# Down-projections of three feed-forward stages: seven block products per four hidden chunks in place of eight

## The chip, the core and the metric

One core of a Trainium2 chip. Its engines are PE (TensorE, the matmuls), DVE (VectorE), ACT (ScalarE), POOL (GpSimd) and SP (SyncE, which here issues the transfers of the weights). The metric is the device time of one launch in microseconds, as the median of the runs.

## What is computed

A stack of three layers over 512 tokens of width 1024, all in fp32. Each layer is a token mixer and then a feed-forward stage, with residuals and root-mean-square norms between. The change bears on the feed-forward stages and on the product `mod`:

```python
def _squared_relu_mlp(x, w1, w2):          # layers 0 and 1: w1 1024x4096, w2 4096x1024
    h = jax.nn.relu(x @ w1)
    return (h * h) @ w2

def swiglu(h, w_ffn_in, w_ffn_out):        # third layer: 1024x5632, 2816x1024
    gate, up = jnp.split(h @ w_ffn_in, 2, axis=-1)
    return (jax.nn.silu(gate) * up) @ w_ffn_out

c_act = jax.nn.silu(c)                     # c 1x1024, for the third layer
mod = c_act @ w_ada[l] + b_ada[l]          # w_ada 1024x6144
```

## The kernel before

**Products.** Every fp32 product runs as three matmuls: each operand is split into a rounded part (hi) and the rest (lo), and `mm3` (L277) issues hi·hi, hi·lo and lo·hi, lines L280 to L282:

```python
mm(out, s[0], m[0], start=start, stop=False)
mm(out, s[0], m[1], start=False, stop=False)
self.gemm = mm(out, s[1], m[0], start=False, stop=stop).ins
```

**Weights.** They come in units of 128x1024 (512 KB) in the order that `plan()` writes down. `unit` (L255) loads one by SP into a tile `wraw`, casts it on ScalarE into `whi` (L267) and subtracts on VectorE into `wlo` (L268). The tiles come from three rings, `RINGS` (L220): 3 raw, 4 hi and 4 lo, from a point in the first mixer on 3 more of hi and lo. A load waits until the subtraction on its slot's last content is through.

**A feed-forward stage** (`ffn`, L1149, for l = 0 and 1). The hidden width of 4096 is taken as 32 chunks of 128, in eight groups of four. `w1()` makes a group: for each chunk 24 matmuls into one PSUM bank (tile `g`; chunk-major, weights stationary), a relu with a scale per token on VectorE (L1168, `g` to `r`), a square on ScalarE (L1169), and `split` into hi and lo (ScalarE L274, VectorE L275) in the tile `a`. `accum_group` (L1190) then adds the group's share of the output into `m` (512 tokens x 1024): for each of two column halves two weight units, for each of four token tiles one bank (tile `a`) of 12 matmuls, which ScalarE copies out in the first group (L1198) and VectorE adds in all others (L1200). The loop makes group g and then projects group g-1 down, so TensorE has 96 matmuls up, 96 down in one round. The last group is projected by `tail`, whose evacuation is woven with the norms that follow.

**The modulation** (`modulation`, L1204) is done beside the first feed-forward stage alone, in seven steps of six or seven tiles of `w_ada` (48 in all, tile `wada`, two buffers of their own): SP loads 512 KB, and VectorE multiplies with `ca` and sums along the row in one instruction (L1220).

**The third stage** (`swiglu`, L1613) has 22 chunks in groups of 2, 4, 4, 4, 4, 4; a chunk takes two units of weights up (a gate and a value). While its last but one group is projected, GpSimd multiplies and adds finished halves of `m` into the residual (`gated`, L1636).

**PSUM** gives the products of these stages four banks, two named `g` and two `o`, taken in turn (`bank`).

**Order.** Each engine runs its own instructions strictly in order. These orders are set when the program is built, by a scheduler that goes by its estimates and the dependences; `issue_after(done)` (L1178) keeps the modulation's loads behind a relu of the round before.

## Time and profile before

| | |
|---|---|
| median of 3 runs | 2073.69 us (2072.18 to 2075.59) |
| profiled execution: its time | 2073.41 us |
| profiled execution: its span | 2071.6 us |
| granted TensorE clock, mean | 0.99 |

The profile shows one execution. Its page gives the busy time of each engine, the chain of work that ended last and the costliest groups of instructions; the trace behind it has the start and the duration of each instruction, what it waited for, and the busy time of each engine in any stretch. In the names, `a<-r` reads "tile a out of tile r", and `x64` counts instructions. Two matmuls after each other overlap in the records, so that the time between their starts, not their durations, tells how fast TensorE goes. A granted clock of 1.00 is the full 2.4 GHz, and the lower level is 1.2 GHz.

### The profile page before, as it was taken

Reading aid. Unit: us, or ns where it says so; the run is one execution under the profiler, and the core shown is the slowest. Engines: PE = TensorE matmul, PEld = TensorE weight load, DVE = VectorE, ACT = ScalarE, POOL = GpSimd, SP = SyncE. Lnnn points to the kernel's source line nnn. Section 1 sums busy time; section 2 is a strip of 40 time slices with the busy share of each in tenths; the row PEclk is TensorE's granted clock in tenths of the full one; section 3 lists DMA queues with packets and bytes.
Section 4 is the critical chain, followed back from the end, with each engine's and each line's share of the span. In section 5 each row is a group of like instructions: output and inputs, shape, how many; then the busy total and the mean of one; then the engine's idle time right before and its main releaser. Section 6 shows DMA issues by size and latency. Waiting matters only on the chain.

```text
span 2071.6 us, 26020 instructions
## 1 busy us (share of the span) xinstructions
PE 2026.2 (98%) x10312; PEld 1713.2 (83%) x10312; DVE 1113.7 (54%) x1698; ACT 801.9 (39%) x1352; POOL 189.5 (9%) x230
## 2 busy tenths in 40 slices
PE   8989999999999999999999999999999999999998
PEld 6767889888888788888888888898888889888886
DVE  7676656666665546665444444633564654243335
ACT  5445555422333534224432322424655434322222
POOL 3212221000002100003000000300000000000006
PEclk9989999999999999999999999999999999999999
DMA  7211043755542332222333223122121222323231
GB/s 251 85 31 42 31 156 110 240 189 196 190 148 77 115 101 94 93 85 72 102 102 102 92 92 102 62 93 91 49 75 62 90 93 92 102 92 98 89 99 41
DMA packets 59691, 213.54 MB, mean 103 GB/s; under 512 B 6952, under 2 KB 7273, under 8 KB 59185
## 3 DMA queue, kind: packets, MB, share of 16 engines
q1 hardware_dynamic: 56592, 202.84, 29.8%
q0 software_dynamic: 1728, 5.28, 0.8%
q10 hardware_dynamic: 1248, 3.76, 0.6%
q8 instruction: 81, 1.33, 0.3%
q14 instruction: 42, 0.34, 0.0%
HBM read 206.59 MB, written 2.10 MB: 101 GB/s over the span
## 4 chain that ended last, share of the span: by engine, by line
PE 90%; DVE 4%; POOL 3%; ACT 2%; issue 1%; DMA 0%; POOLq 0%; SPq 0%; ACTq 0%; DVEq 0%
PE g L280 13%; PE g L282 13%; PE g L281 13%; PE a L282 8%; PE a L280 8%; PE a L281 8%; PE h L281 2%; PE h L280 2%; PE h L282 2%; PE t L280 2%; PE t L281 2%; PE t L282 2%; PE l L280 2%; PE l L282 2%; PE l L281 2%
## 5 line engine op out<-in xcount | busy, mean ns | idle before, releaser
L267 ACT CAST whi<-wraw 128x1024 fp32r<-128x1024 f32 x326 | 340.9, 1048 | 851.3 <-PE g L281 385.3
L268 DVE TENSOR_TENSOR wlo<-wraw,whi 128x1024 fp32r<-128x1024 f32 x326 | 400.6, 1231 | 312.9 <-ACT whi L267 309.2
L280 PE MATMUL g<-a,whi 128*128 128x512 f32 x1200 | 474.3, 395 | 0.0
L281 PE MATMUL g<-a,whi 128*128 128x512 f32 x1200 | 470.5, 392 | 0.0
L282 PE MATMUL g<-a,wlo 128*128 128x512 f32 x1200 | 470.5, 392 | 0.0
L280 PE MATMUL a<-whi,a 128*128 128x512 f32 x688 | 268.3, 390 | 0.0
L281 PE MATMUL a<-wlo,a 128*128 128x512 f32 x688 | 267.8, 389 | 0.0
L282 PE MATMUL a<-whi,a 128*128 128x512 f32 x688 | 267.8, 389 | 0.0
L282 PEld LDWEIGHTS g<-a,wlo 128*128 128x128 f32 x1200 | 226.3, 189 | 46.9
L280 PEld LDWEIGHTS g<-a,whi 128*128 128x128 f32 x1200 | 226.8, 189 | 45.5 <-DVE a L1595 0.2
L281 PEld LDWEIGHTS g<-a,whi 128*128 128x128 f32 x1200 | 226.5, 189 | 45.1
L1200 DVE TENSOR_TENSOR a<-a,a 128x512 f32<-128x512 f32 x168 | 114.4, 684 | 104.1 <-PE a L282 103.6
L282 PEld LDWEIGHTS a<-whi,a 128*128 128x128 f32 x688 | 129.2, 188 | 26.8
L281 PEld LDWEIGHTS a<-wlo,a 128*128 128x128 f32 x688 | 129.2, 188 | 26.6
L280 PEld LDWEIGHTS a<-whi,a 128*128 128x128 f32 x688 | 129.2, 188 | 26.5
L280 PE MATMUL h<-a,whi 128*128 128x256 f32 x384 | 109.9, 290 | 4.4 <-DVE a L540 2.7
L281 PE MATMUL h<-a,whi 128*128 128x256 f32 x384 | 109.8, 287 | 2.2 <-DVE a L597 2.0
L282 PE MATMUL h<-a,wlo 128*128 128x256 f32 x384 | 109.4, 286 | 0.0
L1168 DVE SCALAR_TENSOR_TENSOR r<-g,rbc 128x512 f32<-128x512 f32 x52 | 35.9, 691 | 128.5 <-PE g L282 128.5
L280 PE MATMUL l<-whi,a 128*128 128x512 f32 x256 | 100.8, 394 | 0.0
L282 PE MATMUL l<-whi,a 128*128 128x512 f32 x256 | 99.6, 390 | 0.0
L281 PE MATMUL l<-wlo,a 128*128 128x512 f32 x256 | 99.5, 389 | 0.0
(411 smaller groups left out, 2795.7 us busy)
## 6 DMA issues: line engine op xcount, KB each, us to landing
wraw<-wbig SPq DMA_DIRECT2D x320, 512.0 KB, 3.5
wada<-wada SPq DMA_DIRECT2D x48, 512.0 KB, 4.5
cw<-cmp_w SPq DMA_DIRECT2D x2, 1024.0 KB, 10.2
rowng<-rows POOLq DMA_DIRECT2D x4, 512.0 KB, 5.2
h<-x ACTq DMA_DIRECT2D x1, 2048.0 KB, 11.3
out<-a SPq DMA_DIRECT2D x8, 256.0 KB, 2.2
xin<-xT SPq DMA_DIRECT2D x3, 512.0 KB, 7.4
qt<-qt ACTq DMA_DIRECT2D x12, 128.0 KB, 2.2
```

The source lines that it names most:

```text
L267: nc.scalar.copy(hi[:, :w], raw)
L268: nc.vector.tensor_tensor(lo[:, :w], raw, hi[:, :w].bitcast(F32), ALU.subtract)
L280: mm(out, s[0], m[0], start=start, stop=False)
L281: mm(out, s[0], m[1], start=False, stop=False)
L282: self.gemm = mm(out, s[1], m[0], start=False, stop=stop).ins
L1168: done = nc.vector.scalar_tensor_tensor(r, o, 0.0, rb, ALU.max, ALU.mult).ins
L1200: nc.vector.tensor_add(t, t, o)
```

## The change

Four hidden chunks (a group) times 1024 columns are a product of two by two blocks: tokens in two halves of 256 by hidden chunks in two pairs, and hidden pairs by column halves. Strassen's scheme in Winograd's form takes seven block products and block sums where the plain way takes eight. The class `Winograd` does this for a stage:

- The hidden blocks stay F32 in a region `ys` (two groups); blocks and their sums are split into a ring of four slots of hi and lo.
- The seven products run in the order 1: a11·b11, 2: a12·b21, 5: s1·t1, 3: s4·b22, 6: s2·t2, 7: s3·t3, 4: a22·t4, each of two banks with six matmuls per bank. Each product has an accumulator of 128x2x512: four lie in `m`, and products 1, 6 and 7 have tiles of their own (`acc`).
- The sums of hidden blocks (s1 to s4, tile `yt`, 128x512) and of weight blocks (t1 to t4, tile `wt`, 128x1024) run on GpSimd, from the raw tiles. The casts and subtractions of the weights follow on these sums.
- After the last group but one, `join` forms the result's blocks from the accumulators, with five sums on GpSimd and two on VectorE; the last group of each stage is still projected by `tail` in the plain way. In the third stage the groups are 4, 4, 4, 4, 2, 4, and `group` serves the first four; the group of two runs as before.
- The modulation's tiles come from the raw ring and have no `issue_after`. Its product is a GpSimd multiplication and a ScalarE copy that sums along the row.
- The rings of hi and lo grow by 2 in place of 3, and the raw ring grows from 3 to 5.

```diff
-RINGS = (("raw", 3), ("hi", 4), ("lo", 4)), (("hi", 3), ("lo", 3))
+RINGS = (("raw", 3), ("hi", 4), ("lo", 4)), (("raw", 2), ("hi", 2), ("lo", 2))
...
             for g in range(1, 8):
-                *yn, after = w1()
-                self.accum_group("w2", y, m, g == 1)
-                y = yn
+                w1(g)
+                down.group(g - 1, g == 7)
                 if l == 0:
-                    with tc.issue_after(done):
-                        self.modulation(g)
-                done = after
+                    self.modulation(g)
...
         for j in range(lo, hi):
-            w = self.ada.tile([P, D], F32, tag="w", name="wada")
+            w = self.turned("raw").tile([P, D], F32, tag="w", name="wada")
             nc.sync.dma_start(w, a["wada"][j])
-            nc.vector.scalar_tensor_tensor(w, w, 1.0, self.ca, ALU.mult, ALU.mult, accum_out=self.mod[:, j:j + 1])
+            nc.gpsimd.tensor_tensor(w, w, self.ca, ALU.mult)
+            nc.scalar.activation(w, w, AF.Copy, accum_out=self.mod[:, j:j + 1])
...
+class Winograd:
...
+    def group(self, g, last):
+        k, nc = self.k, self.k.nc
+        y = self.y(g)
+        a11, a12, a21, a22 = (y[:, 2 * c:2 * c + 2, i * 256:i * 256 + 256] for i in range(2) for c in range(2))
+
+        def sub(a, b, n, op=ALU.subtract):
+            t = self.temp(self.wk, "yt" if n == 256 else "wt", n)
+            nc.gpsimd.tensor_tensor(t, a, b, op)
+            return t
+
+        def product(p, a, b):
+            a, b = self.pair(a), k.parts(b)
+            for i in range(2):
+                o = k.bank(k.ps, f"a{p}{i}_")
+                for _ in k.token_major(o, [([b], Kernel.stationary(a))], i):
+                    pass
+                t = self.acc[p][:, i]
+                if g == 0:
+                    nc.scalar.copy(t, o)
+                else:
+                    nc.vector.tensor_add(t, t, o)
+
+        b11, b21 = k.raw_unit(self.tag), k.raw_unit(self.tag)
+        s1 = sub(a21, a22, 256, ALU.add)
+        product(1, a11, b11)
+        s2 = sub(s1, a11, 256)
+        product(2, a12, b21)
+        b12 = k.raw_unit(self.tag)
+        t1 = sub(b12, b11, 512)
+        product(5, s1, t1)
+        s4 = sub(a12, s2, 256)
+        b22 = k.raw_unit(self.tag)
+        t2 = sub(b22, t1, 512)
+        product(3, s4, b22)
+        product(6, s2, t2)
+        s3 = sub(a11, a21, 256)
+        t3 = sub(b22, b12, 512)
+        t4 = sub(t2, b21, 512)
+        product(7, s3, t3)
+        product(4, a22, t4)
+        if last:
+            self.join()
+
+    def join(self):
+        nc, acc = self.k.nc, self.acc
+        nc.gpsimd.tensor_tensor(acc[2], acc[2], acc[1], ALU.add)
+        nc.gpsimd.tensor_tensor(acc[6], acc[6], acc[1], ALU.add)
+        nc.gpsimd.tensor_tensor(acc[7], acc[7], acc[6], ALU.add)
+        nc.vector.tensor_tensor(acc[6], acc[6], acc[5], ALU.add)
+        nc.vector.tensor_tensor(acc[3], acc[3], acc[6], ALU.add)
+        nc.gpsimd.tensor_tensor(acc[4], acc[7], acc[4], ALU.subtract)
+        nc.gpsimd.tensor_tensor(acc[5], acc[5], acc[7], ALU.add)
```

How the orders of the engines change is shown for a late round of the first stage, in which the weight blocks are `wraw_5324` (b11), `wraw_5326` (b21), `wraw_5376` (b12) and `wraw_5404` (b22). Line numbers are those of the kernel named.

GpSimd, the change, one round: `yt` are sums of hidden blocks, `wt_5378` is t1, `wt_5406` t2, `wt_5454` t3, `wt_5456` t4, and `wada` the modulation's products.

```order
L1736 TENSOR_TENSOR yt_5328<-a_3543 128x512
L1736 TENSOR_TENSOR yt_5352<-yt_5328,a_3543 128x512
L1736 TENSOR_TENSOR yt_5402<-a_3543,yt_5352 128x512
L1736 TENSOR_TENSOR wt_5378<-wraw_5376,wraw_5324 128x1024
L1736 TENSOR_TENSOR wt_5406<-wraw_5404,wt_5378 128x1024
L1736 TENSOR_TENSOR wt_5454<-wraw_5404,wraw_5376 128x1024
L1226 TENSOR_TENSOR wada<-wada,ca 128x1024 x2
L1736 TENSOR_TENSOR yt_5452<-a_3543 128x512
L1226 TENSOR_TENSOR wada<-wada,ca 128x1024 x2
L1736 TENSOR_TENSOR wt_5456<-wt_5406,wraw_5326 128x1024
L1226 TENSOR_TENSOR wada<-wada,ca 128x1024 x3
L1736 TENSOR_TENSOR yt_5667<-a_3543 128x512
```

Before, GpSimd has no instruction in such a round. Now it has eight sums and seven products, all seven products behind t2 and the last three behind t4.

ScalarE, before, the same place (casts of the down weights, squares, and the hi part of hidden chunks):

```order
L267 CAST whi_5322<-wraw_5321 128x1024
L1169 ACTIVATE r<-r 128x512
L274 CAST a_5017<-r 128x512
L267 CAST whi_5358<-wraw_5357 128x1024
L1169 ACTIVATE r<-r 128x512
L274 CAST a_5017<-r 128x512
L267 CAST whi_5394<-wraw_5393 128x1024
```

ScalarE, the change, the same round (L1227 are the copies that sum the modulation's products, L1180 the squares, L272 the casts of weight blocks and sums):

```order
L1227 ACTIVATE wada,mod<-wada 128x1024 x2
L272 CAST whi_5382<-wt_5378 128x1024
L1180 ACTIVATE a_3543<-a_3543 128x512
L1227 ACTIVATE wada,mod<-wada 128x1024 x3
L272 CAST whi_5410<-wraw_5404 128x1024
L1180 ACTIVATE a_3543<-a_3543 128x512
L1227 ACTIVATE wada,mod<-wada 128x1024 x2
L272 CAST whi_5432<-wt_5406 128x1024
L1180 ACTIVATE a_3543<-a_3543 128x512
L272 CAST whi_5460<-wt_5454 128x1024
```

The seven copies of one round stand ahead of the cast of that round's t2; the last two of them stand directly ahead of it. They read the seven GpSimd products of the fence above: before this cast ScalarE has 41 copies in its order, and GpSimd has 34 products ahead of t2 and 41 behind the round's last.

VectorE, the change, from the lo part of t2 on (L1179 relu, L273 lo of a weight, L281 lo of a hidden block, L1749 additions from PSUM):

```order
L273 TENSOR_TENSOR wlo_5433<-wt_5406,whi_5432 128x1024
L1179 SCALAR_TENSOR_TENSOR a_3543<-g_79_5297,rbc_2972 128x512
L273 TENSOR_TENSOR wlo_5461<-wt_5454,whi_5460 128x1024
L1749 TENSOR_TENSOR acc_37_3546<-acc_37_3546,a_81_5336 128x512
L1749 TENSOR_TENSOR acc_37_3546<-acc_37_3546,a_81_5344 128x512
L281 TENSOR_TENSOR a_3544<-yt_5352,a_3544 128x512
L273 TENSOR_TENSOR wlo_5483<-wt_5456,whi_5482 128x1024
L1749 TENSOR_TENSOR a_3545<-a_3545,a_81_5360 128x512
L1749 TENSOR_TENSOR a_3545<-a_3545,a_81_5368 128x512
L281 TENSOR_TENSOR a_3544<-yt_5452,a_3544 128x512
L1749 TENSOR_TENSOR a_3545<-a_3545,a_82_5386 128x512
L273 TENSOR_TENSOR wlo_5534<-wraw_5531,whi_5533 128x1024
```

It goes on with two additions, a split, the lo part `wlo_5567` of the second up-weight, two additions and the lo part `wlo_5600` of the third up-weight of the next round; the slot that `wlo_5600` reads, `wraw_5597`, is the one into which the next round's b22 is loaded. Before, the lo parts of the down weights stood in VectorE's order beside the modulation's own products (L1220) and waited for casts of raw units alone. On PE the order has 9395 rows before and 9179 with the change.

## Rows read from the trace of the kernel before

**Rows 1.** The page, section 1: busy time, share of the span and instructions of each engine.

```profile
PE 2026.2 (98%) x10312; PEld 1713.2 (83%) x10312; DVE 1113.7 (54%) x1698; ACT 801.9 (39%) x1352; POOL 189.5 (9%) x230
```

**Rows 2.** The page, section 4: the chain that ended last, by engine.

```profile
PE 90%; DVE 4%; POOL 3%; ACT 2%; issue 1%; DMA 0%; POOLq 0%; SPq 0%; ACTq 0%; DVEq 0%
```

**Rows 3.** Timeline, VectorE: start us, us, engine line op out<-in [idle before <-releaser].

```profile
481.43 0.69 DVE L1168 SCALAR_TENSOR_TENSOR r<-g,rbc 128x512 f32<-128x512 f32 x1 [2.76 <-PE g L282]
...
524.95 0.69 DVE L1168 SCALAR_TENSOR_TENSOR r<-g,rbc 128x512 f32<-128x512 f32 x1 [2.76 <-PE g L282]
```

**Rows 4.** Busy time by stretch: one period of the first feed-forward stage.

```profile
core 0: us, PE busy (x) PEld busy (x) DVE busy (x) ACT busy (x) POOL busy (x), PEclk, DMA share, GB/s
481.43:524.95 43.52, 43.52 (x193) 36.05 (x192) 27.96 (x40) 13.05 (x17) 0.00 (x0) 1.00 0.54 179
```

**Rows 5.** Groups by form, VectorE: line engine op, shapes xcount | busy us, mean ns | idle before.

```profile
L268 DVE TENSOR_TENSOR wlo<-wraw,whi 128x1024 fp32r<-128x1024 f32 x320 | 395.0, 1237 | 309.6 <-ACT whi L267 305.9
L1200 DVE TENSOR_TENSOR a<-a,a 128x512 f32<-128x512 f32 x168 | 114.4, 684 | 104.1 <-PE a L282 103.6
L1220 DVE SCALAR_TENSOR_TENSOR wada<-wada,ca 128x1024 f32<-128x1024 f32 x48 | 58.0, 1221 | 16.4 <-DMA wada<-wada 16.1
L275 DVE TENSOR_TENSOR a<-r,a 128x512 fp32r<-128x512 f32 x64 | 45.9, 725 | 1.2 <-ACT a L274 1.2
L1168 DVE SCALAR_TENSOR_TENSOR r<-g,rbc 128x512 f32<-128x512 f32 x52 | 35.9, 691 | 128.5 <-PE g L282 128.5
```

**Rows 6.** Groups by form, ScalarE.

```profile
L267 ACT CAST whi<-wraw 128x1024 fp32r<-128x1024 f32 x320 | 336.0, 1052 | 847.2 <-PE g L281 384.9 <-PE a L282 292.6 <-issue 66.3
L1169 ACT ACTIVATE r<-r 128x512 f32<-128x512 f32 x64 | 39.6, 625 | 4.2 <-DVE r L1168 4.2
L274 ACT CAST a<-r 128x512 fp32r<-128x512 f32 x64 | 39.3, 620 | 1.7
L494 ACT ACTIVATE junk<-h 128x1024 bf16<-128x1024 f32 x20 | 21.2, 1058 | 53.7 <-DVE h L551 38.2 <-DVE h L1607 12.7 <-issue 2.7
...
L494 ACT ACTIVATION_READ_ACCUMULATOR junk<-a 128x1 f32 x32 | 6.1, 190 | 0.0
```

**Rows 7.** Groups by form, GpSimd.

```profile
L1638 POOL TENSOR_TENSOR a<-a,row 128x512 f32<-128x512 f32 x8 | 10.3, 1290 | 319.7 <-DVE a L1200 319.6
...
L1237 POOL TENSOR_TENSOR ws<-ws,consts 128x1024 f32<-128x1024 f32 x1 | 2.4, 2387 | 3.9 <-DMA ws<-wsT 3.9
```

**Rows 8.** DMA issues: KB each, median us to landing.

```profile
wraw<-wbig SPq DMA_DIRECT2D x320, 512.0 KB, 3.5
wada<-wada SPq DMA_DIRECT2D x48, 512.0 KB, 4.5
```

**Rows 9.** Timeline, VectorE and GpSimd around 677 us.

```profile
677.14 2.35 DVE L268 TENSOR_TENSOR wlo<-wraw,whi 128x1024 fp32r<-128x1024 f32 x2
...
677.37 3.27 POOL L547 TENSOR_TENSOR mg<-a,rowng 128x512 f32<-128x512 f32 x1 [2.67 <-DVE a L540]
...
679.57 2.16 DVE L268 TENSOR_TENSOR wlo<-wraw,whi 128x1024 fp32r<-128x1024 f32 x1
...
680.61 2.24 POOL L554 TENSOR_TENSOR a<-a,rowng 128x512 f32<-128x512 f32 x1
```

**Rows 10.** Timeline, VectorE and GpSimd around 2045 us.

```profile
2044.88 1.28 POOL L1639 TENSOR_TENSOR h<-h,a 128x512 f32<-128x512 f32 x1
...
2044.98 1.73 DVE L1651 TENSOR_TENSOR h<-h,a 128x512 f32<-128x512 f32 x1
...
2046.79 1.29 POOL L1653 TENSOR_TENSOR a<-h,rownfin 128x512 f32<-128x512 f32 x1 [0.63 <-DVE h L1651]
...
2046.98 0.69 DVE L1650 TENSOR_TENSOR a<-l,row 128x512 f32<-128x512 f32 x1 [0.27 <-PE l L282]
```

**Rows 11.** Busy time by stretch, with PEclk, where TensorE had little to do.

```profile
83.00:87.00 4.00, 1.28 (x5) 1.10 (x6) 3.75 (x14) 2.21 (x8) 3.49 (x10) 0.88 0.01 4
87.00:91.00 4.00, 4.00 (x14) 3.22 (x14) 2.78 (x6) 1.20 (x3) 2.68 (x4) 0.69 0.30 74
```

More of the change, by code (lines that the diff above doesn't have):

```diff
@@ L149, in fi @@
             split4("fi", "w_ffn_in_2", 0, np.concatenate([_r(0), _r(DFF), _r(P), _r(DFF + P)]))
-            return
-        for i in range(4 * g - 2, 4 * g + 2):
+        for i in ((2, 3), range(4, 8), range(8, 12), range(12, 16), (16, 17), range(18, 22))[g]:
             fm("fg", "w_ffn_in_2", 0, _r(i * P))
@@ L513, in mod_row @@
     def mod_row(self, k, pool=None):
-        g = (pool or self.rows).tile([P, D], F32, tag="row", name=f"row{k}")
+        g = (pool or self.rows).tile([P, D], F32, tag="row", name=f"row{k}", bufs=1)
         for c in range(2):
@@ L1189, in accum_group @@
         nc = self.nc
+        kc, y = y[0].shape[1], self.stationary(y)
         for c in range(2):
-            ws = [self.unit(tag) for _ in range(y[0].shape[1] // 2)]
+            ws = [self.unit(tag) for _ in range(kc // 2)]
             for i in range(NT):
@@ L1639, in gated @@
                 nc.gpsimd.tensor_tensor(self.h[:, i, cs], self.h[:, i, cs], m[:, i, cs], ALU.add)
[L1641 removed]
+            fi(0)
             for g in range(1, 6):
[L1643 to L1645 removed]
+                fi(g)
+                if g < 5:
+                    down.group(g - 1, g == 4)
+            self.accum_group("fo", down.pairs(4, 2), m, False, gated)
             ss, col = self.cols4("ssm"), self.cols4("col")
@@ L1664, in swiglu @@
             ws = [[self.unit("fo") for _ in range(2)] for c in range(2)]
+            y = down.whole(5)
             tail = self.tail([(c, [(ws[c], y)]) for c in range(2)], evac)
@@ L1668, in swiglu, with __init__, block, y @@
                     pass
+class Winograd:
+    def __init__(self, k, wk, region, tag):
+        self.k, self.wk, self.tag = k, wk, tag
+        self.ys = k.region(region, F32)
+        self.ring = k.region(region)
+        self.slot = 0
+        self.m = k.tokens()
+        def block(i, c):
+            return self.m[:, 2 * i:2 * i + 2, c * 512:c * 512 + 512]
+        self.acc = {2: block(0, 0), 3: block(0, 1), 4: block(1, 0), 5: block(1, 1)}
+        for p in (1, 6, 7):
+            self.acc[p] = wk.tile([P, 2, 512], F32, name=f"acc{p}_{k.pos}", bufs=1)
+    def y(self, g):
+        return self.ys[:, 4 * (g % 2):4 * (g % 2) + 4]
+    def pair(self, src):
+        s = self.slot
+        self.slot = (s + 1) % 4
+        hi, lo = self.ring[:, s], self.ring[:, 4 + s]
+        if len(src.shape) == 3:
+            hi, lo = (t.rearrange("p (k t) -> p k t", k=src.shape[1]) for t in (hi, lo))
+        self.k.split(hi, lo, src)
+        return hi, lo
+    def pairs(self, g, n):
+        y = self.y(g)
+        self.slot = 0
+        for i in range(n):
+            self.pair(y[:, i])
+        return self.ring[:, :n], self.ring[:, 4:4 + n]
+    def whole(self, g):
+        y = self.y(g)
+        ps = [self.pair(y[:, i]) for i in range(4)]
+        return lambda k, i: tuple(t[:, i * P:(i + 1) * P] for t in ps[k])
+    def temp(self, pool, tag, n):
+        return pool.tile([P, 2, n], F32, tag=tag, name=f"{tag}{self.k.pos}", bufs=3)
+    def group(self, g, last):
+        k, nc = self.k, self.k.nc
+        y = self.y(g)
+        a11, a12, a21, a22 = (y[:, 2 * c:2 * c + 2, i * 256:i * 256 + 256] for i in range(2) for c in range(2))
[43 more added lines that the diff above has]
+        nc.gpsimd.tensor_tensor(acc[5], acc[5], acc[7], ALU.add)
```

83 lines of the change are left out of this document (40 added, 43 removed).

## The prediction, made before the changed kernel was run

> **What bounds the kernel now.** I read the page first: TensorE is busy for 98% of the span [rows 1], and the chain that ended last is 90% PE [rows 2]. So the question for any edit is what it does to the number of matmuls, and whether TensorE is still fed. Then I read one steady period of the first feed-forward stage (four hidden chunks up, four down). The evictions of the same unit in two following periods start at 481.43 and 524.95 [rows 3], 43.52 us apart. In this period 192 matmuls of 512 columns are issued (96 up, 96 down), which is 0.2267 us each; the matmul durations of the page overlap and can't be summed. In the same stretch PE is busy throughout, VectorE 27.96 us, ScalarE 13.05 us and GpSimd not at all [rows 4]. The others hide wholly under TensorE, with a third of VectorE's time and all of GpSimd's free.
>
> **What goes.** A group of four chunks costs 84 matmuls in place of 96 (seven products of 12). There are 7 + 7 + 4 such groups in the three stages, so 18 x 12 = 216 matmuls go, 216 x 0.2267 = **-49.0 us**; no other part of the change removes TensorE time. A period of a feed-forward stage would then be 180 x 0.2267 = 40.8 us.
>
> **What comes, per group.** VectorE: 11 lo subtractions of weights (4 up, 7 down; 8 before) at 1.237, 7 splits of hidden blocks (4 before) at 0.725, 14 additions from PSUM (8 before) at 0.684, 4 relu at 0.691 [rows 5]: 13.6 + 5.1 + 9.6 + 2.8 = 31.1 us. It loses the modulation's products, 48 x 1.221 in all [rows 5]. ScalarE: 11 casts at 1.052, 7 at 0.620, 4 squares at 0.625, and in the first stage seven accumulating copies, which are nearest to the 1024-wide square with its accumulator read, 1.058 + 0.190 [rows 6]: 27.1 us. GpSimd: four 512-wide sums at 1.290 and four 1024-wide ones at 2.387, the only such row [rows 7]: 14.7 us; in the first stage also seven modulation products of 128x1024, 16.7 us, together 31.4. Every sum is under 40.8. If sums decided, all would be hidden.
>
> **Why I don't believe the sums in the first stage.** Queues run in order, and there the order makes a ring. ScalarE has all seven accumulating copies ahead of the cast of the weight sum t2 (see the order of ScalarE above). The last of these copies needs the last GpSimd product of the group, which stands behind all of that group's sums. So from one "last modulation product" to the next, these follow each other, with nothing to shorten them:
> - ScalarE: accumulating copy 1.25, cast of t2 1.05 [rows 6]: 2.3 us.
> - VectorE, in its order from lo of t2 up to lo of the next group's third up-weight: six lo x 1.237, nine additions x 0.684, three splits x 0.725, one relu 0.69 [rows 5]: 16.5 us. Behind the waiting lo stand the evictions that free PSUM banks, so TensorE, which has four banks, stands too.
> - SP (the queue of the loads): only now is the slot of that up-weight free for block b22: 3.5 us to land [rows 8].
> - GpSimd: t2, t3, t4 and seven modulation products, ten x 2.387, and one hidden sum 1.29 [rows 7]: 25.2 us.
>
> The sum is **47.4 us** with no contention. The GPSIMD Engine Reference of the Trainium skill (section Elementwise) gives 4497 ns for an fp32 tensor_tensor of 2048 columns and advises VectorE for such work; halved, an estimate of 2.25 us per product, which would make the ring 46.0 and the time 8 us less. The row of this trace, 2.387, decides.
>
> **Contention.** Two VectorE subtractions started at 677.14 and 679.57; a GpSimd product started in between took 3.27 us in place of 1.29, and the third subtraction 2.16 in place of 1.23 [rows 9]. Likewise h+a on VectorE took 1.73 us beside a GpSimd sum, ending 0.55 after that, and an operation that reads PSUM took its usual 0.69 [rows 10]. So two-input SBUF operations of the two engines exclude each other: what a subtraction holds is 1.09 us for 1024 columns and 0.55 for 512. In the ring GpSimd's three other hidden sums, 3 x 1.29 = 3.9 us, can stand in VectorE's part, and four lo and four splits of VectorE, 4 x 1.09 + 4 x 0.55 = 6.6, in GpSimd's part. Bounds: 0 and 10.5 us. I take half of the first, since additions from PSUM run beside them, and of the second all but one lo and one split, which fit under the transfer: 1.9 + 4.9 = 6.8. **Period 54.2 us**, between 47.4 and 57.9.
>
> **The sum.** Six such rings lie between the modulation steps of the first stage: 6 x (54.2 - 40.8) = +80.4 (39.6 to 102.6). The first group waits for its own six products: GpSimd has four hidden sums, four weight sums and six products, 4 x 1.29 + 10 x 2.387 = 29.0 us, in sequence, of which I let some 17 lie under the up-projection before it (21.8 us): +12 (5 to 20). At the end of a stage the block accumulators are joined: after the last but one pair of additions come two GpSimd sums and, on VectorE in front of the last splits of the hidden chunks, two 1024-wide sums, an addition and three splits, 4.8 + 2.5 + 0.7 + 2.2 = 10.2 us, against two banks (2.7) and 16 matmuls (3.6) that TensorE still has: +4 where GpSimd is free (second stage), +5 in the first, +1 in the third, where a whole up-projection of 8 units lies over it (0 to 8 each).
>
> Second stage: no modulation, so GpSimd has 14.7 us of 40.8. During the 84 matmuls (19.0 us) VectorE has 14 additions, six lo and five splits, 20.6 us; the four banks let it lag 5 us, which covers 1.6, but three GpSimd sums begin just there. Bounds: 0, and all of GpSimd's 14.7 less VectorE's idle 9.7 = 5 a group. I take 1, nearest to the first since most GpSimd sums fall in the up-projection: 7. Third stage: the same with a longer up-projection, 0.75 a group: 3.
>
> TensorE will stand for some 13 us in each ring; where it was busy 1.28 of 4 us, its granted clock fell to 0.69 in the next 4 us [rows 11], the lower level for part of it. I cost this at nothing: a product of 12 matmuls at 1.2 GHz takes 5.4 us, VectorE's share of the ring has about as much for one, and TensorE is banks ahead; without this cover it is up to 2 us a ring. The rings of weights shrink from 7 to 6 (casts, subtractions) and grow from 3 to 5 (loads); the other stages hold a unit for 24 matmuls, 5.4 us, so six are 33 us ahead of a chain of 3.5 + 1.05 + 1.24: nothing; without it 5.8 us a unit. The SP queue now has the next up-weights behind the seven modulation loads, the last of which waits for t4; that lies under the two GpSimd products left then, 4.8 us. POOL's queue has the evacuation's products and a row load behind the joins; they are in the terms for the ends.
>
> 2073.4 (the profiled execution; the median is 2073.69, 0.3 above it) - 49.0 + 80.4 + 12 + 5 + (7 + 4) + (3 + 1) = **2137 us**.
>
> **Rivals.**
> - The waits are met early and only sums count, since ScalarE's copies come in time: the first stage behaves like the second, 7 + 5. 2024.4 + 12 + 11 + 4 = 2051, faster. It decides as soon as the ring is under 40.8, for which GpSimd's 1024-wide product would have to take 1.7 us. For it: all sums are under 40.8. Against it: the only 1024-wide row says 2.387, and the order is strict.
> - The ring holds, but the exclusion costs nothing there: 47.4 a period, 2137 - 40.8 = 2096.
> - The exclusion costs all it can, 57.9: 2159. The page SBUF — State Buffer of the Trainium skill (section Who interferes with whom) says that such an operation holds the shared ports for its whole instruction; by that rule the holds are 1.24 and 0.73, the ring is 59.2 and the time 2167. Rows 10 show 0.55 of 0.69 held.
> - VectorE becomes the bound of the other two stages as well, 5 us in each of the 11 groups in place of 10 in all: 2182.
> - That the change does less than it says I exclude: the instruction order of PE has 216 rows fewer.
>
> **How the numbers follow.** Forecast (ring 51 to 57) 0.50; ring near 47 0.17; ring near 58 0.15; faster 0.12; all stages bound 0.06. The range leaves out the faster case and the last one: from the ring at 47.4 with the lower bounds of the rest, 2024.4 + 39.6 + 5 = 2069, taken as 2070, to the ring at 57.9 with start and ends at their upper bounds, 2159 + 8 + 8 = 2175. About 0.2% (4 us) is what a measurement of this kernel can tell from no change. Faster 0.12; same 0.03, the foot of the second case; slower 0.85.
>
> **What would show it.** In the profile after: GpSimd's modulation product at 2.4 us or more x48; the relu of the same unit 50 to 58 us apart in the first stage and 41 to 43 in the second; gaps of PE in the first stage ended by VectorE's relu and additions, with VectorE waiting for ScalarE and that for GpSimd; a granted clock under 1.0 only in the first stage. A period of 41 in the first stage would make the ring wrong; one of 47, the contention.

## The result, and the profile after

The changed kernel takes **2138.82 us** in the median of 4 runs (2137.75 to 2141.34), the kernel before 2073.69: a ratio of 1.0315 with a 95% interval of 1.0297 to 1.0333. It is slower by 3%. The profiled execution took 2139.02 us with a span of 2137.2. The forecast was 2137.

The page's first and fourth sections, of the changed kernel, answer to [rows 1] and [rows 2]:

```profile
PE 2008.2 (94%) x10096; PEld 1688.8 (79%) x10096; DVE 1376.0 (64%) x1806; ACT 940.2 (44%) x1574; POOL 689.2 (32%) x437
```

```profile
PE 71%; DVE 12%; POOL 10%; issue 3%; ACT 3%; DMA 1%; SPq 0%; POOLq 0%; DVEq 0%; ACTq 0%
```

TensorE has 216 instructions fewer and 18 us less busy time, but it is busy for 94% of a longer span; VectorE and GpSimd now hold 12% and 10% of the chain that ended last. The time is lost in the first feed-forward stage and at the ends of the stages. The relu on VectorE marks the places (timeline, VectorE, changed kernel; columns as in [rows 3]): the stage's first and last relu, and between them one unit's relu in two following rounds, for the first stage and then for the second.

```profile
351.60 2.47 DVE L1179 SCALAR_TENSOR_TENSOR a<-h,rbc 128x512 f32<-128x512 f32 x4
...
537.72 0.69 DVE L1179 SCALAR_TENSOR_TENSOR a<-g,rbc 128x512 f32<-128x512 f32 x1
...
590.64 0.68 DVE L1179 SCALAR_TENSOR_TENSOR a<-g,rbc 128x512 f32<-128x512 f32 x1
...
698.58 0.68 DVE L1179 SCALAR_TENSOR_TENSOR a<-g,rbc 128x512 f32<-128x512 f32 x1
...
1074.75 2.47 DVE L1179 SCALAR_TENSOR_TENSOR a<-h,rbc 128x512 f32<-128x512 f32 x4
...
1162.60 0.68 DVE L1179 SCALAR_TENSOR_TENSOR a<-g,rbc 128x512 f32<-128x512 f32 x1
...
1203.39 0.68 DVE L1179 SCALAR_TENSOR_TENSOR a<-g,rbc 128x512 f32<-128x512 f32 x1
...
1335.90 0.69 DVE L1179 SCALAR_TENSOR_TENSOR a<-g,rbc 128x512 f32<-128x512 f32 x1 [3.28 <-PE g L288]
```

The first stage's rounds are 590.64 - 537.72 = **52.92 us** apart where [rows 3] had 43.52; the second stage's 1203.39 - 1162.60 = **40.79**, just the 180 matmuls that are left. Busy time by stretch shows what fills the two rounds (columns as in [rows 4]):

```profile
537.72:590.64 52.92, 43.75 (x180) 35.65 (x180) 37.95 (x38) 24.82 (x37) 37.17 (x15) 0.89 0.45 149
1162.60:1203.39 40.79, 40.79 (x182) 33.77 (x181) 35.96 (x37) 17.50 (x23) 18.70 (x8) 1.00 0.32 104
```

With the same products and sums TensorE works through the second round without a gap. In the first it stands for 9.2 us. The groups of GpSimd, which answer to [rows 7], show the modulation's product at 2.77 us in the mean and the weight sums at 2.65 to 3.16, where the one row of before said 2.387:

```profile
L1226 POOL TENSOR_TENSOR wada<-wada,ca 128x1024 f32<-128x1024 f32 x48 | 132.0, 2770 | 4.8 <-DMA wada<-wada 3.7 <-issue 1.0
...
L1736 POOL TENSOR_TENSOR wt<-wraw,wraw 128x1024 f32<-128x1024 f32 x36 | 113.6, 3155 | 114.2 <-DMA wraw<-wbig 114.2
...
L1736 POOL TENSOR_TENSOR wt<-wraw,wt 128x1024 f32<-128x1024 f32 x18 | 47.7, 2651 | 35.2 <-DMA wraw<-wbig 34.3
```

**The ring in the trace.** The timelines of ScalarE, VectorE and GpSimd over one round of the first stage:

```profile
536.46 1.06 ACT L1227 ACTIVATE wada<-wada 128x1024 f32<-128x1024 f32 x1 [1.95 <-POOL wada L1226]
...
537.52 1.03 ACT L272 CAST whi<-wt 128x1024 fp32r<-128x1024 f32 x1
...
538.63 1.23 DVE L273 TENSOR_TENSOR wlo<-wt,whi 128x1024 fp32r<-128x1024 f32 x1 [0.22 <-issue]
...
550.56 1.21 DVE L273 TENSOR_TENSOR wlo<-wraw,whi 128x1024 fp32r<-128x1024 f32 x1
...
555.52 3.18 POOL L1736 TENSOR_TENSOR wt<-wraw,wraw 128x1024 f32<-128x1024 f32 x1 [7.75 <-DMA wraw<-wbig]
...
558.78 2.74 POOL L1736 TENSOR_TENSOR wt<-wraw,wt 128x1024 f32<-128x1024 f32 x1
...
573.25 5.82 POOL L1226 TENSOR_TENSOR wada<-wada,ca 128x1024 f32<-128x1024 f32 x2
...
581.38 7.97 POOL L1226 TENSOR_TENSOR wada<-wada,ca 128x1024 f32<-128x1024 f32 x3
...
590.56 0.17 DVE L1228 TENSOR_TENSOR mod<-mod,vecs 128x7 f32<-128x7 f32 x1 [3.41 <-ACT wada L1227]
```

At 536.46 ScalarE starts the last copy of a round, released by GpSimd's product, and right behind it (537.52) the cast of t2. VectorE subtracts t2's lo part at 538.63 and comes to the lo part of the second up-weight at 550.56, in its order and without a pause. Only then the slot is free for block b12, which GpSimd awaits (`<-DMA wraw<-wbig`) and has at 555.52. Then GpSimd runs t1, t2, t3, the products, t4 and the last three products, to 581.38 + 7.97 = 589.35. At 590.56 VectorE's bias addition of the round has waited 3.41 us for ScalarE's copy, and with it the relu behind it. The wait that holds TensorE's weight loads longest in the whole program, in total, is the one put down to these copies (us in total, times, longest):

```profile
PEld a L286 <- ACT wada L1227: 39.1, 5, 10.2
```

The matmuls' own record of this round puts the same stand down to the cast behind the copies (PE from ACT whi L272, 9.8 us).

**Where all of it went.** Between equal instructions of the two traces (before, the first stage's first and last relu stand at 349.74 and 628.30, the second's at 997.08 and 1275.64), with 12 x 0.2267 = 2.72 us of matmuls credited per group:

| place | forecast | measured | how |
|---|---|---|---|
| before the first stage | 0 | +1.9 | first relu 349.74 to 351.60; it stands between 349.25 and 351.05 in runs 2, 5, 6, 7 and 10 |
| start of the first stage | +12 | +16.9 | 68.4 longer from first to last relu, + 16.3 of matmuls = 84.7, less the rings |
| six rings | +80.4 | +67.8 | last products end at 382.66 and 695.23: 312.6 - 6 x 40.8 |
| end of the first stage | +5 | +9.0 | shift 70.3 at the last relu, 76.5 at the end of the norm behind it, + 2.7 |
| second stage, rounds | +7 | -1.1 | shift 77.7 to 60.3, + 16.3 |
| second stage, end | +4 | +10.4 | shift 60.3 to 67.9, + 2.7 |
| third stage, rounds | +3 | +0.1 | shift 68.1 to 57.3, + 10.9 |
| third stage, end | +1 | +8.4 | shift 57.3 to 65.7 in the last evacuation |
| matmuls | -49.0 | -49.0 | 216 instructions |

The remaining 1.4 us lie in the mixers between. The forecast's 63.4 stands against 65.6 measured. The total is closer than its terms, and that is luck: 13 us too much in the rings and 11 in the later rounds stand against 23 too little at the start and at the three ends.

The end of the second stage (timelines of GpSimd and VectorE, then busy time by stretch, columns as in [rows 4]):

```profile
1356.54 2.71 POOL L1776 TENSOR_TENSOR acc<-acc,acc 128x1024 f32<-128x1024 f32 x1 [1.82 <-DVE acc L1749]
...
1359.28 1.23 DVE L1777 TENSOR_TENSOR acc<-acc,a 128x1024 f32<-128x1024 f32 x1 [1.69 <-POOL acc L1776]
...
1361.02 2.99 DVE L1778 TENSOR_TENSOR a<-a,acc 128x1024 f32<-128x1024 f32 x1
...
1363.94 4.03 DVE L281 TENSOR_TENSOR a<-a,a 128x512 fp32r<-128x512 f32 x3
```

```profile
1360.00:1364.00 4.00, 0.83 (x3) 0.19 (x1) 4.00 (x4) 0.00 (x0) 3.41 (x2) 0.93 0.00 0
1364.00:1368.00 4.00, 1.18 (x3) 0.99 (x4) 4.00 (x5) 0.00 (x0) 2.22 (x1) 0.50 0.00 0
1368.00:1372.00 4.00, 4.00 (x15) 3.15 (x14) 2.89 (x4) 0.72 (x2) 0.21 (x1) 0.71 0.40 125
```

VectorE waits 1.69 us for a join on GpSimd (1356.54), does its own two sums, the second of them in 2.99 us in place of 1.2, and only then the three splits (4.03 us in place of 2.2) without which the stage's last projection can't start. TensorE works for 2.0 of the 8 us from 1360 to 1368; its granted clock is 0.93, then 0.50, the lower of its two levels (1.2 GHz), and 0.71 in the next stretch, in which it is busy throughout.

The end of the third stage (timelines of VectorE and GpSimd):

```profile
2099.13 0.67 DVE L1208 TENSOR_TENSOR a<-a,a 128x512 f32<-128x512 f32 x1
...
2111.91 1.29 POOL L1644 TENSOR_TENSOR h<-h,a 128x512 f32<-128x512 f32 x1
...
2116.22 0.48 DVE L1665 TENSOR_SCALAR a<-a,col 128x512 f32<-128x512 f32 x1 [8.34 <-POOL col L517]
```

The last addition of the group of two chunks (VectorE, out of TensorE's last bank) is done at 2099.80; GpSimd is still gating finished halves until 2113.2, then multiplies two halves by the norm's row, and VectorE, in the last evacuation, has waited 8.34 us for it.

### The profile page after: what moved, and what is told of

The parts are those of the page before. It is cut to its first block, busy times and chain, and to the rows that moved or that the text cites. A ratio compares the mean times of both kernels' runs of the same rounds, so it can differ in the third digit from the quotient of the medians.

```text
span 2137.2 us, 26461 instructions
## 1 busy us (share of the span) xinstructions
PE 2008.2 (94%) x10096; PEld 1688.8 (79%) x10096; DVE 1376.0 (64%) x1806; ACT 940.2 (44%) x1574; POOL 689.2 (32%) x437
## 4 chain that ended last, share of the span: by engine, by line
PE 71%; DVE 12%; POOL 10%; issue 3%; ACT 3%; DMA 1%; SPq 0%; POOLq 0%; DVEq 0%; ACTq 0%
PE g L286 11%; PE g L288 11%; PE g L287 11%; PE a L286 5%; PE a L287 4%; PE a L288 4%; POOL wada L1226 4%; DVE wlo L273 4%; PE t L286 2%; PE t L287 2%; PE t L288 2%; PE h L287 2%; PE h L288 2%; PE h L286 2%; DVE a L281 2%
## 5 line engine op out<-in xcount | busy, mean ns | idle before, releaser
L273 DVE TENSOR_TENSOR wlo<-wraw,whi 128x1024 fp32r<-128x1024 f32 (+2 forms) x308 | 467.1, 1518 | 253.5 <-ACT whi L272 251.0
L272 ACT CAST whi<-wraw 128x1024 fp32r<-128x1024 f32 (+2 forms) x308 | 321.0, 1045 | 357.2 <-PE g L287 195.3
L286 PE MATMUL a<-whi,a 128*128 128x512 f32 x616 | 249.1, 404 | 63.3 <-ACT whi L272 34.7
L287 PE MATMUL a<-wlo,a 128*128 128x512 f32 x616 | 246.7, 401 | 0.0
L288 PE MATMUL a<-whi,a 128*128 128x512 f32 x616 | 246.4, 400 | 0.0
L1736 POOL TENSOR_TENSOR wt<-wraw,wraw 128x1024 f32<-128x1024 f32 x36 | 113.6, 3155 | 114.2 <-DMA wraw<-wbig 114.2
L273 DVE TENSOR_TENSOR wlo<-wt,whi 128x1024 fp32r<-128x1024 f32 x72 | 102.2, 1420 | 50.8 <-ACT whi L272 48.7
L1226 POOL TENSOR_TENSOR wada<-wada,ca 128x1024 f32<-128x1024 f32 x48 | 132.0, 2770 | 4.8 <-DMA wada<-wada 3.7
L272 ACT CAST whi<-wt 128x1024 fp32r<-128x1024 f32 x72 | 75.2, 1045 | 116.5 <-PE g L287 100.9
L1736 POOL TENSOR_TENSOR yt<-a 128x512 f32<-128x512 f32 x36 | 57.9, 1610 | 201.3 <-DVE a L1637 80.3
L288 PE MATMUL l<-whi,a 128*128 128x512 f32 x256 | 101.5, 401 | 14.3 <-DVE a L281 14.3
```

Of the source, the lines that this page charges most:

```text
L272: self.nc.scalar.copy(hi, raw)
L273: self.nc.vector.tensor_tensor(lo, raw, hi.bitcast(F32), ALU.subtract)
L1226: nc.gpsimd.tensor_tensor(w, w, self.ca, ALU.mult)
L1736: nc.gpsimd.tensor_tensor(t, a, b, op)
```

## The experiments

Times of a single run stand without an interval. The runs came in four batches (1 to 4, 5 to 8, 9 to 11, 12); the kernel before, on the same chips, had medians of 2072.1, 2075.0, 2073.8 and 2073.9 us beside them, so that single runs of two batches can differ by 3 us for nothing. Where a step is small, equal instructions of the two traces are compared.

**1. The modulation's product back on VectorE.**

```diff
-            nc.gpsimd.tensor_tensor(w, w, self.ca, ALU.mult)
-            nc.scalar.activation(w, w, AF.Copy, accum_out=self.mod[:, j:j + 1])
+            nc.vector.scalar_tensor_tensor(w, w, 1.0, self.ca, ALU.mult, ALU.mult, accum_out=self.mod[:, j:j + 1])
```

> The changed kernel with the modulation's product back on VectorE as one instruction with its row sum, as before the change; no GpSimd product, no ScalarE copy. Theory (the ring through ScalarE's copies sets the 52.9 us period of the first stage): the ring is gone; VectorE has 31.1 + 7 x 1.22 = 39.7 us of work against 40.8 of matmuls, so the period is 40.8 to 44 and the time 2055 to 2085. Rival (GpSimd's block sums beside VectorE, or the scheme itself, make the period): it stays over 50 and the time over 2115.

Measured: 2091.8 us, a period of 46.5, a little above the theory's range and far under the rival's. One round:

```profile
509.94:556.49 46.55, 43.95 (x180) 35.83 (x180) 44.59 (x52) 17.30 (x22) 19.23 (x8) 0.93 0.52 172
```

VectorE is busy for 44.6 of 46.6 us, 4.9 above the 39.7 of its rows: its subtractions and two of its products are stretched beside GpSimd's block sums, which the expectation had left out. The rest is one wait of 1.96 us for a tile to land. So without ScalarE's copies and GpSimd's products more than half of what the modulation costs (2138.8 against 2053.5 in run 2) is gone, and VectorE is the next bound.

**2. No modulation at all.** The loop over the tiles is left out.

> The changed kernel without the modulation's loads, products and row sums (mod is the bias alone, so the output is not the reference's). Theory: the first stage runs like the second, period 40.8; 2138.8 less 78.9 (six rings of 52.9 and one of 59) less some 6 at the start, 2054, between 2048 and 2060. Rival (the cost is in the block sums, not in the modulation): over 2100.

Measured: 2053.5, a period of 40.80, as the theory said:

```profile
484.46:525.26 40.80, 40.80 (x181) 33.80 (x180) 35.98 (x37) 17.49 (x23) 18.85 (x8) 1.00 0.32 102
```

Eight block sums a round on GpSimd and 36 us on VectorE hide completely. The scheme costs nothing in this stage's rounds by itself.

**3. The copies behind the casts on ScalarE.** `down.cast` is the cast of t3.

```diff
-                    self.modulation(g)
+                    with tc.issue_after(down.cast):
+                        self.modulation(g)
```

> The changed kernel with one thing moved: the seven accumulating copies of a round stand behind the casts of that round's t2 and t3 on ScalarE, in place of ahead of them. All work is as in the change. Theory (the order closes the ring): the period falls to 41 to 45 us, the time to 2060 to 2091. Rival A (what bounds is the exclusion: GpSimd's 31.4 us and the 15.8 us that VectorE's subtractions hold can't run at once, 47.2 in sum): a period of 47 or more, 2100 to 2110. Rival B (the order does not matter): 2139.

Measured: 2123.6, a period of 49.9. Nearest is rival A, but the time lies between A and B. Of the 12.1 us that a round takes over 40.8, 3.0 come back:

```profile
521.68:571.57 49.89, 42.67 (x180) 33.16 (x180) 49.56 (x39) 24.18 (x36) 39.26 (x16) 1.00 0.50 159
```

```profile
525.61 2.81 DVE L273 TENSOR_TENSOR wlo<-wt,whi 128x1024 fp32r<-128x1024 f32 x1
```

VectorE now runs back to back, 49.56 of 49.89 us, on the 31.1 us of work that [rows 5] gave it: its 1024-wide subtractions take 2.8 us beside GpSimd's products. But more changed than the order on ScalarE, and the ring is not gone. The scheduler also put two of GpSimd's products behind the next round's s2, and the copies, no longer ahead of the cast of t2, now stand ahead of the casts of the up-weights (timelines of ScalarE and GpSimd):

```profile
539.78 1.06 ACT L1228 ACTIVATE wada<-wada 128x1024 f32<-128x1024 f32 x1 [1.65 <-POOL wada L1227]
...
540.84 2.94 ACT L272 CAST whi<-wraw 128x1024 fp32r<-128x1024 f32 x3
...
549.95 2.39 POOL L1737 TENSOR_TENSOR wt<-wraw,wraw 128x1024 f32<-128x1024 f32 x1 [8.51 <-DMA wraw<-wbig]
```

VectorE's subtraction of the second up-weight ends at 545.46, its slot's next load is issued at 545.49, and GpSimd, which has waited 8.51 us for it, starts t1 at 549.95. So the same ring still closes, over the casts of the up-weights in place of that of t2. Order and contention are both tight in this run, and it doesn't tell what either costs by itself.

**4. The moved modulation alone, in the kernel before.** Its product and copy as in the change, its own two buffers kept.

> The kernel before with the modulation's product moved to GpSimd and its row sum to ScalarE, and nothing else. Theory: alone this part is hidden, since no cast waits for GpSimd there and GpSimd has 16.7 us of 43.5: 2070 to 2078. Rival (a GpSimd product beside VectorE's subtractions costs by itself, through what they hold): 2090 or more.

Measured: 2112.2, a clear miss of the theory. It is no contention either: GpSimd's products take 2.48 us in the mean. The rounds with modulation take 56 to 58 us, those behind it 43.52 again:

```profile
475.11:531.01 55.90, 47.25 (x187) 37.89 (x188) 27.75 (x27) 28.02 (x45) 34.31 (x15) 0.91 0.62 208
...
573.05:616.57 43.52, 43.52 (x193) 36.04 (x192) 20.40 (x27) 13.05 (x17) 0.00 (x0) 1.00 0.30 97
```

The timelines of GpSimd and ScalarE show why:

```profile
494.14 2.40 POOL L1220 TENSOR_TENSOR wada<-wada,ca 128x1024 f32<-128x1024 f32 x1 [1.81 <-DMA wada<-wada]
...
496.57 1.06 ACT L1221 ACTIVATE wada<-wada 128x1024 f32<-128x1024 f32 x1 [3.06 <-POOL wada L1220]
...
497.62 1.98 ACT L267 CAST whi<-wraw 128x1024 fp32r<-128x1024 f32 x2
```

There are two buffers, each goes through load, product and copy before its next load may start, and ScalarE's copies, waiting for these products, stand ahead of casts of weights (the cast at 497.62 starts when the copy ahead of it, 3.06 us late, is through). The chain of that round has 45% in loads of `wada` and 29% in the products. Here too a row sum on ScalarE behind a GpSimd product is a wait in the queue of the casts, without any of Strassen's sums. What more buffers would give back was not tried. That the theory held this to be hidden was a sum of busy times, the very thing that the prediction had warned of.

**5. The modulation beside the mixer.** One VectorE instruction a tile, six tiles for each of four column chunks and four in each of six rounds of the gated mixer.

> The changed kernel with the whole modulation (one VectorE instruction a tile, as before the change, raw ring) taken out of the first feed-forward stage and put beside the gated mixer that follows it, where VectorE is busy for 16 of 24 us a step and GpSimd for 0.5. Theory (seven blocks cost nothing in a stage where neither the ring nor GpSimd's products stand against the subtractions): both feed-forward stages have periods of 40.8 us, and the time is that of the run without modulation, 2053.5, plus 0 to 5. Rival (48 products more on VectorE, or on the raw ring, delay the mixer): over 2065.

Measured: 2059.9; both stages have rounds of 40.8:

```profile
484.49:525.29 40.80, 40.80 (x181) 33.80 (x180) 35.99 (x37) 17.49 (x23) 18.92 (x8) 1.00 0.33 103
```

The price of the modulation there is 6.3 us against run 2, of another batch. Between equal instructions it is 5.4, a little over the theory's upper bound: from the first stage's last relu to the second's first it is 382.2 us against 376.8 in run 2, and 4.2 of the difference are there by the end of the mixer's first chunk.

**6. The joins behind the splits.**

```diff
-        if last:
-            self.join()
...
             y = down.whole(7)
+            down.join()
```

> As the run with the modulation in the mixer, and the joins of the two first stages emitted behind the splits of the last hidden chunks. Theory (at a stage's end TensorE waits for splits that stand behind the join's two sums on VectorE; 9.0 and 10.3 us lost at the two ends): 14 to 19 us less than that run, 2036 to 2042. Rival (the wait only moves: the evacuation of the last group needs the joined blocks, and TensorE runs out of banks): under 6 us less.

Measured: 2057.7, only 2.2 less, and between equal instructions nothing: from the first stage's first relu to the second's it is 643.6 us against 643.5 in run 5, from the second stage's last relu to the last product of gate and value in the third 752.5 against 752.3. The rival holds: the splits come earlier, but the norm behind them still waits for the joins on GpSimd.

**7. The gating in the tail.**

```diff
-                nc.vector.tensor_tensor(t, o, row[:, cs], ALU.mult)
+                nc.vector.tensor_add(t, t, o)
+                nc.vector.tensor_tensor(t, t, row[:, cs], ALU.mult)
```

and no GpSimd work on finished halves.

> As the run with the late joins, and in the third stage no gating of half-finished sums on GpSimd: the last evacuation adds the sum from m to the bank and then multiplies and adds as before (one more VectorE instruction for each of eight halves). Theory (at the end 16 GpSimd instructions of 1.3 us follow a group of two chunks, whose 48 matmuls take 10.9 us, and the last evacuation waits 8.4 us for them): 6 to 8 us less than that run, 2029 to 2035, faster than the kernel before by some 2%. Rival (the additions lengthen the last evacuation by as much): within 3 us of that run.

Measured: 2050.2 (4 runs, 2046.2 to 2052.2), 7.5 less than run 6; against the kernel before 0.9877, interval 0.9861 to 0.9894. The step is as large as expected (6.2 of it lie behind the third stage's last product of gate and value), the total higher because run 6 had not given what it should. At the second stage's end TensorE is still held up: from 1278 to 1282 us its granted clock is 0.50 and seven matmuls fill 3.26 us.

**8. More GpSimd work that nobody reads.** Seven products `extra = extra * extra` a round in the second stage.

> The changed kernel with seven more GpSimd products of 128x1024 in each round of the second feed-forward stage, on a scratch tile that nothing reads: no load, no copy, nobody waits for them. There the period is 40.8 us now. Theory of exclusion (GpSimd's 31.4 us and the 15.8 us that VectorE's SBUF subtractions hold add up to 47.2): the period goes to 46 to 50, the time to 2170 to 2195. Theory of the ring alone (GpSimd has 40.8 us for 31.4 of work, and no one waits for the extra work): the period stays under 42, the time under 2148.

Measured: 2212.6, but the run doesn't answer the question. Nothing bound the products to their rounds; GpSimd's order has them in front of the first stage's joins, and the second stage's rounds were as before, 40.80 us from one relu (1239.83) to the same of the next round (1280.63). GpSimd's timeline:

```profile
696.46 3.87 POOL L1193 TENSOR_TENSOR extra<-extra 128x1024 f32<-128x1024 f32 x2
```

**9. The same, bound to their rounds** by an edge to s4, s3 and t4.

> The run with extra GpSimd products again, this time bound to places in each round of the second feed-forward stage: three behind s4, one behind s3, three behind t4, where GpSimd stands idle now; still nobody reads them. Theory of exclusion (31.4 us of GpSimd and 15.8 held by VectorE's subtractions add up to 47.2): the period of that stage goes from 40.8 to 46 to 50 us, the time to 2170 to 2195. Theory of the ring alone: no cast and no copy waits for these products, so the period stays under 42 and the time under 2148.

Measured: 2166.4; two rounds of the second stage take 88.6 us, 44.3 each, between the two theories:

```profile
1179.86:1268.47 88.61, 84.35 (x361) 68.33 (x360) 82.10 (x72) 34.98 (x45) 72.19 (x31) 0.98 0.30 95
```

What TensorE's matmuls waited for in these two rounds (us in total, times, longest):

```profile
PE a L286 <- DVE a L1759: 4.3, 3, 2.1
```

Nobody reads these products, yet a round is 3.5 us longer. Of the 7.0 us in these two rounds TensorE stands for 4.3, each time until a VectorE addition is done, and the rest are matmuls at the lower clock behind the stands. Another explanation would be that the block sums come late, since they stand behind the extra products in GpSimd's queue; but VectorE waits only 0.7 us in the two rounds for casts. So contention is real, but its price is not the plain sum of 47.2. It depends on what meets: VectorE was busy for 41 us a round here and 49.6 in run 3, with the same work of its own.

**10. The joins on VectorE alone**, added to run 7.

```diff
-        nc.gpsimd.tensor_tensor(acc[2], acc[2], acc[1], ALU.add)
+        nc.vector.tensor_tensor(acc[2], acc[2], acc[1], ALU.add)
```

and so on for all five.

> As the run with the gating in the tail (2050.2), and all seven sums of each join on VectorE in place of five on GpSimd. Theory (at the two first stages' ends the wait moved because the last splits and the join's two VectorE sums are stretched by GpSimd's sums beside them, and the norm's GpSimd products stand behind those): VectorE's seven sums are 8.6 us against 21.8 us of matmuls left, 5 to 10 us less, 2040 to 2046. Rival (VectorE becomes the engine that is late there): no gain or a loss.

Measured: 2045.1 in one run, as expected; the fastest version of this study, 1.4% under the kernel before in the same batch. It is 5.1 under the median of run 7 and 1.1 under the lowest of its four. Between equal instructions the gain lies behind the second stage alone: from the first stage's first relu to the second's last it is 904.4 us against 904.1 in run 7, from there to the third stage's last product of gate and value 746.6 against 751.8. At the first stage's end, one of the two places where the theory looked for it, nothing is gained. What is left shows at the end of the first stage (timelines of GpSimd and VectorE, and busy time by stretch):

```profile
635.52 7.14 POOL L566 TENSOR_TENSOR a<-a,rowng 128x512 f32<-128x512 f32 x1 [32.16 <-ACT junk L506]
```

```profile
636.87 1.22 DVE L1775 TENSOR_TENSOR acc<-acc,a 128x1024 f32<-128x1024 f32 x1
```

```profile
650.00:654.00 4.00, 0.00 (x0) 0.00 (x0) 4.00 (x6) 2.21 (x6) 2.21 (x2) 0.61 0.43 133
```

The norm's GpSimd product, 1.3 us elsewhere, takes 7.14, while five VectorE operations of 1.22 (the lo subtraction of a weight and four joins) run one behind the other beside it, to 641.50, and what stands behind it in the norm starts only then. The same product takes 7.13 at the second stage's end of this run (1278.61), and at the same place in runs 11 (636.42) and 12 (636.59). The chain of waits from 628 to 662 has 28% in such products (L566), the largest share of a line there; TensorE has nothing to do from 650 to 658.

**11. The modulation held behind each chunk's statistics**, added to run 10 with `issue_after`.

> As the run with the joins on VectorE, and the modulation's products of each column chunk of the mixer held behind that chunk's statistics on VectorE, so that none stands among the norm at the end of the first feed-forward stage. Theory (the modulation in the mixer cost 6.3 us against leaving it out, most of it before the mixer's first chunk): 2 to 5 us less than the run with the joins on VectorE; 2036 to 2043, faster than the kernel before by 1.5 to 1.8%. Rival (its price lies in the mixer's rounds): no change from that run.

Measured: 2091.9 (5 runs), 1.0086 of the kernel before, interval 1.0072 to 1.0099: 47 us worse than run 10, which neither theory foresaw. The chain of waits, changed as described, and a stretch:

```profile
727.74 2.37 DVE wada L1225 x4
730.13 4.51 DMA wraw<-wbig
734.66 1.05 ACT whi L272
```

```profile
720.00:740.00 20.00, 10.57 (x38) 7.84 (x37) 11.72 (x18) 5.17 (x6) 0.00 (x0) 0.77 0.48 164
```

The tiles share the raw ring with the weights. Held back to the end of a chunk, they hold back the loads of the next chunk's weights too: a product, then the load (4.5 us), the cast, and TensorE works for 10.6 of 20 us. It is a ring again, built by one edge: the next chunk's statistics are released by these matmuls, and its four products start at 761.83, 34.1 us later.

**12. The modulation from the second chunk on**, by the order of the code alone, added to run 10.

> As the run with the joins on VectorE (2045.1), with the modulation of the mixer begun one column chunk later by the order of the code: eight tiles behind each of the second to fourth chunk's weights in the raw ring in place of six behind each of the four, the silu of c behind the first chunk's; nothing is held back by an edge, so no weight waits for statistics. Theory (six tiles, ca and its three activations stand among the norm at the end of the first feed-forward stage, where TensorE stands for 11 us): 2 to 5 us less, 2040 to 2043, faster than the kernel before by 1.5%. Rival (what TensorE waits for there is GpSimd's product of the norm, stretched by VectorE's join sums, and not the modulation): within 2 us of 2045.

Measured: 2055.7 (4 runs), 0.9909 of the kernel before, interval 0.9892 to 0.9925, some 10 us worse than run 10, which neither theory foresaw. At the mixer's first chunk next to nothing is gained: its last matmuls stand at 694.6 us against 694.0 in run 10, whose first stage began 1.2 earlier. TensorE's matmuls there wait for the norm's sums on VectorE for 12.5 us, in run 10 for 12.6, so the stand at the end of the stage is not the modulation's, as the rival said. The loss comes in the mixer: from the first stage's last relu to the second's first it is 388.9 us against 381.8. With eight tiles a chunk VectorE waits 6.5 us between 755 and 775 for tiles to land (0.6 in run 10), with the last chunk's statistics behind them, and TensorE is busy for 13.69 us from 760 to 780, in run 10 for 19.11:

```profile
760.00:780.00 20.00, 13.69 (x55) 11.15 (x54) 15.71 (x31) 9.51 (x13) 2.53 (x2) 0.83 0.58 190
```

## Why the prediction was right, and where its steps were off

- **The matmuls** (-49.0) went as counted, 216 by the page.
- **The ring** was the likeliest case, and it is what the trace shows: 52.9 us a round against 54.2. Its terms: ScalarE 2.2 us (forecast 2.3). The step "in its order from lo of t2 up to lo of the next group's third up-weight" entered one load too late: GpSimd waited for b12, freed by the second up-weight, so that VectorE's part is 13.1 (forecast 16.5, with contention 18.4) and t1 belongs to GpSimd's part. The load is 3.75 (3.5). GpSimd's part is 33.8, of which eleven products and sums of 2.387 and one of 1.29 are 27.55 by [rows 7], and 6.3 are stretch and short waits; the forecast had 25.2 + 4.9. With the prediction's own prices this ring is 2.3 + 13.84 + 3.5 + 27.55 = 47.2 without contention, where the forecast had 47.4: the miscount cancels by luck. What came on top is 5.7; the allowance was 6.8.
- GpSimd's short waits in its part, 0.88 us for a tile and 0.69 for a split on VectorE before s3 at 571.68, show that a second path, VectorE's own order up to that split, is as long as the one through the load. Both end in the same products and copies.
- The lower clock was costed at nothing, and that holds in this round: the granted clock is 0.89 in it, but VectorE has no pause between 538.63 and 551.77, so that it waits for no product there.
- Only five of the six rings are of this length; the first, 382.66 to 430.50, is 47.8, with the first group's evictions on ScalarE. That and 1.3 us a ring are the 12.6 too much in this term.
- **Every sum is under 40.8, and still it did not hide**: runs 2 and 5, with rounds of 40.8, bear out that the modulation, not the scheme, is at fault. Stretched as they are, VectorE is busy for 37.95 and GpSimd for 37.17 of the 52.92 us, so contention alone does not make the round; and the same GpSimd load costs 3.5 us where nobody reads its results (run 9), not 12.1. By the sum above, 6.4 of the 12.1 would stand without contention. That is a sum and no run shows it: no run kept all the work and was free of a ring, since in run 3 it closed over another cast. How the 12.1 divide stays open.
- **Contention** was bounded by what operations hold (1.09 and 0.55 us) and by [rows 9, 10]. The Trainium skill, SBUF — State Buffer, section Who interferes with whom, says that a VectorE instruction with two inputs in SBUF contends with a GpSimd instruction that reads SBUF, and that the order of issue, not the shape of the operations, decides which of the two is blocked. Run 10 agrees in kind, with 7.14 us for a product of 1.3; that a chain of VectorE operations stays ahead over five instructions is shown by the run and not said by the Trainium skill. The measured ring, 52.9, is well under the 59.2 us that the rule of whole instructions would have given, but does not test it: the 59.2 also takes for granted that all these operations meet.
- **The rounds of the other stages** were costed at 1 and 0.75 us a group; they cost nothing. VectorE was stretched to 36 us as feared (31.1 by [rows 5]), under 40.8 of matmuls.
- **The ends** were the weak step: +5, +4 and +1 for 9.0, 10.4 and 8.4. "Two GpSimd sums and, on VectorE in front of the last splits, two 1024-wide sums" was the right place, but the cover of 6.3 us did not hold: the sums stretched each other, and from 1364 TensorE's clock was at its lower level. At the third stage's end the term is another one altogether: the change made the last but one group two chunks short, and the gating's 21 us on GpSimd no longer fit under 10.9 us of matmuls. The sum of that stage named POOL's queue, and did not cost it.
- **The faster rival** (2051) is what the kernel does without modulation in this stage: run 2 gave 2053.5.
- What was to show it came in the main: 48 products of 2.77 us in the mean, rounds of 52.9, VectorE waiting for ScalarE and that for GpSimd. TensorE's stands ended otherwise than said: between 382 and 696 us three end with the cast behind the copies (25.7 us), two with a relu (19.8), one with a copy out of PSUM (5.5) and none with an addition. A second stage of 41 to 43 came out at 40.8, and the clock also fell at the second stage's end.
- The upper edge of the range, 2175, adds 8 us for the ends. By the prediction's own bounds, up to 8 at each of three ends where 5, 4 and 1 were taken, it is 14, and the edge 2181.

## What to carry to other kernels

A new instruction in an in-order queue is costed by what stands behind it, not by its microseconds: here a copy of 1.25 us in front of a cast tied four queues into a ring of 52.9 us a round, though no engine had over 40.8 us of work in it, and in run 11 one ordering edge cost 47 us. Follow a waiting instruction through all the queues it passes, the slots of the load ring among them, until it comes back to itself; if it does, the sum along the way is the period. And when a stage changes its last groups, cost its end anew: what was hidden under a long group is not hidden under a short one.

## What the runs showed that was not expected

- A GpSimd product of 128x512 that takes 1.3 us alone took 7.14 beside a chain of five 1024-wide VectorE operations, while these took their usual 1.22 each (run 10, and 7.13 in runs 11 and 12). In the changed kernel, with gaps between them, both sides were stretched: weight sums on GpSimd to 3.16 us, VectorE's subtractions to 3.4.
- The same work of VectorE beside the same number of GpSimd operations kept it busy for 41 us a round in run 9 and for 49.6 in run 3: when the operations meet matters, and not only how many they are.
- At the second stage's end TensorE, busy for 0.83 of 4 us, was granted 0.50 in the next 4 us and 0.71 in the 4 us behind these, in which it was busy again.
